# The summing DMA of a weight pair is issued four products after its loads, and its block is loaded first

## The chip, the core and the metric

The kernel runs on one core of a Trainium2 chip. The core has five engines that run side by side: TensorE (PE) multiplies, VectorE (DVE) and ScalarE (ACT) do the element-wise work, GpSimd (POOL) does a little of it and issues one kind of DMA, and SyncE (SP) issues nearly all other DMAs. Each engine works through its own queue in order and waits there for semaphores. The metric is the device time of one execution in microseconds (us), as the median over runs.

## The reference, cut to what matters

A trunk of four residual layers over 512 tokens of width 1024, in float32: pooling mixer, gated convolution, latent attention, pooling mixer. Nearly all of the time goes into products of the normalized activations with weight matrices; these three lines hold most of the weights:

```python
u, z = jnp.split(xn @ w_in, 2, axis=-1)        # pool_mixer, w_in 1024 x 4096, twice
b, c, h, z = jnp.split(xn @ w_in, 4, axis=-1)  # conv_mixer, w_in 1024 x 8192
h = xn @ w_in                                  # mla_mixer,  w_in 1024 x 2752
```

Each mixer ends in `(mixed * silu(z)) @ w_out` and is added to `x`; a last `rms_norm` closes the trunk.

## The kernel before

**Arithmetic.** Every float32 operand is split into a high part (a copy by ACT, rounded) and a low part (a subtraction by DVE); a product takes three matmuls (high x high, high x low, low x high), so every weight tile costs one ACT and one DVE pass before PE can read it.

**Chunks and pairs.** The work is a list of jobs in a `Stream`. A CHUNK job loads one weight tile of 128 x 1024 floats (`load_chunk`, 512 KB), splits it (`prepare_chunk`, L245 and L248) and multiplies it. A PAIR job computes two output tiles at once with seven products instead of eight (`seven`, by a Strassen-like scheme), from four quarter blocks of the weights and sums of them. There are 52 pairs: 6 in the first pooling layer, 30 in the convolution, 8 in attention's input projection, 8 in the last pooling layer. Each product of a pair is 12 matmuls of 256 columns; a chunk's tile is 24 matmuls of 512 columns.

**What a pair loads.** `load_pair` (L113 to L121) takes three tiles: `r` (1024 columns, L116), `r4` (512 columns, L117, named wq) and `s13` (1024 columns, shown as `s`). `s13` is to hold two sums. Two DMAs put the same quarter block into its two halves (L119, 256 KB each); then a DMA on GpSimd's queue (L120) reads the 512 KB of `r`'s source once more and adds them to `s13` in flight. That adding DMA must wait until both loads of `s13` have landed. `r` and `s13` are buffers of the same tag (wr, four buffers, which the chunks use too); `r4` has two buffers of its own.

**What is done with it.** `prepare_pair` hands the split out over two steps, by positions: position 4 ACT copies `r` (tile ah, L393), position 5 DVE subtracts (al, L396) and ACT copies `s13` (sh), position 6 DVE subtracts (sl) and ACT copies `r4` (ch), position 7 DVE makes cl and two further sums (`sums`, L399 and L400: the last reader of `s13`), positions 10 and 11, that is 2 and 3 of the next step, the copies and subtractions for th and tl (the last readers of `r`).

**What sets the order.** `Stream.step` runs job j. It first loads jobs j+1 and j+2 that are not loaded yet, then puts the preparation of job j+1 into a table of steps, `now`, and runs the job, which calls `now(0)`, `now(1)`, ... between its products: each call executes the entries up to that position. What is left is moved to the next step by minus 8. So a pair is loaded two steps ahead of its products and split in the step before them. PE, DVE and ACT execute in exactly that order (`manual_schedule`, ORDERED in L38). SP's and GpSimd's queues are not in that list: the tile framework orders them and hands out the buffers at compile time, so that an instruction may stand in the queue ahead of one that the code issues before it.

**What else is on GpSimd.** A 16-column memset per convolution tile (L714), the window sums of the pooling layers (`add` in `post_u`, L617, one to four per tile), sums of squares (L282), the power -1/2 of the norms (`rows`, L300), and the scaling of the softmax in attention (L1032).

Of the kernel before, what the change touches and what calls it, by code (L numbers as in the profile page):

```python
# [9 lines left out]
F32 = mybir.dt.float32  # L10
# [3 lines left out]
ALU = mybir.AluOpType  # L14
PSUM = bass.MemoryType.PSUM

P = 128
S = 512
# [15 lines left out]
CH = 1024  # L34
# [30 lines left out]
def trunk_kernel(ctx: ExitStack, tc: tile.TileContext, a):  # L65
    nc = tc.nc
    cp = ctx.enter_context(tc.tile_pool(name="cp", bufs=1))
    wp = ctx.enter_context(tc.tile_pool(name="wp", bufs=1))
# [6 lines left out]
    def nm(s):  # L75
        cnt[0] += 1
        return f"{s}_{cnt[0]}"
# [4 lines left out]
    def wt(s, tag, dt=F32R, w=CH):  # L82
        return wp.tile([P, CH], dt, tag=tag, name=nm(s), bufs=BUFS[tag])[:, :w]
# [10 lines left out]
    def f(t):  # L94
        return t.bitcast(F32)
# [16 lines left out]

    def load_pair(src):  # L113

        r, r4, s13 = wt("wr", "wr", F32), wp.tile([P, S], F32, tag="wq", name=nm("wq"), bufs=2), wt("s13", "wr", F32)
        nc.sync.dma_start(r, src[:, :CH])  # L116
        nc.sync.dma_start(r4, src[:, CH + S :])  # L117
        for q in range(2):
            nc.sync.dma_start(s13[:, q * S : (q + 1) * S], src[:, CH : CH + S])  # L119
        nc.gpsimd.dma_start(s13, src[:, :CH], accum_op=ALU.add)  # L120
        return r, r4, s13  # L121

    raw0 = {}

# [39 lines left out]
    class Steps:  # L164
# [3 lines left out]
        def __init__(self, at=()):  # L168
            self.at = dict(at)
# [15 lines left out]
    class Stream:  # L185
# [1 line left out]


        def __init__(self):
            self.jobs, self.at, self.later, self.raw, self.ready = [], 0, Steps(), {}, {}  # L190

        def add(self, kind, src, run):
            self.jobs.append((kind, src, run))
# [1 line left out]
        def load(self, j):  # L195
            if j < len(self.jobs) and j not in self.raw:
                kind, src, _ = self.jobs[j]
                self.raw[j] = kind[0](src) if kind else None

        def prepare(self, j):  # L200
            if j >= len(self.jobs) or j in self.ready:
# [12 lines left out]
        def step(self):  # L214
            j = self.at
            self.at += 1
            self.load(j + 1)
            self.load(j + 2)
            now, self.later = self.later, Steps()
            now.put(self.prepare(j + 1), 2 if self.jobs[j][0] is PAIR and self.jobs[j + 1 :] and self.jobs[j + 1][0] is not PAIR else 0, first=True)  # L220
            self.jobs[j][2](self.ready.pop(j, None), now)
            now(7)
            left, self.later = self.later, Steps()
            self.later.put(now.at, -8)
            self.later.put(left.at)
# [7 lines left out]
    def load_chunk(src, width=CH):  # L233
        raw = wt("wr", "wr", F32, width)
        nc.sync.dma_start(raw, src)
        return raw

    def prepare_chunk(raw, width=CH, pool=False):
        h, l = wt("wh", "wh", w=width), wt("wl", "wh", w=width)

        def high():
            if pool:
                nc.gpsimd.tensor_scalar(out=h, in0=raw, scalar1=1.0, scalar2=1.0, op0=ALU.mult, op1=ALU.mult)
            else:
                nc.scalar.activation(h, raw, AF.Copy)  # L245

        def low():
            (nc.gpsimd if pool else nc.vector).tensor_tensor(out=l, in0=raw, in1=f(h), op=ALU.subtract)  # L248

        return (h, l), {1: [high], 2: [low]}  # L250

    def wchunk(src, width=CH, pool=False):
        w, steps = prepare_chunk(load_chunk(src, width), width, pool)
        Steps(steps)(2)
        return w

# [129 lines left out]
    def prepare_pair(raw):  # L386
# [15 lines left out]
        def part(h, l, q):  # L402
# [6 lines left out]
                   11: [low(r[:, S:], th[:, :S], tl[:, :S]), low(r4, th[:, S:], tl[:, S:])]}  # L409

    PAIR, CHUNK = (load_pair, prepare_pair), (load_chunk, prepare_chunk)

    def product(w, xf, what, form, out, begin=False, end=False, after=None):
# [382 lines left out]
    def mla_layer(stream, xn, begin, cos_sin, nxt):  # L796
# [140 lines left out]
        def first_k(w, now):  # L937
# [7 lines left out]
            qk[0] = hold.pop("q0"), split(pk, "k")  # L945

        NARROW = (lambda src: load_chunk(src, 768)), (lambda raw: prepare_chunk(raw, 768))
        for i in range(KD):
            ly.pair(stream, a["mla_z"][i], (post_z, post_z), lambda i=i: then(i))
# [8 lines left out]
        def values(g):  # L958
            wh, wl = wchunk(wv[g])
            for tk in range(NT):  # L960
                pv = ps("pv")
                for k in range(2):
                    ts_ = slice(tk * P, (tk + 1) * P)
                    xh, xl = kvl[k]
                    c = slice(k * S, (k + 1) * S)
                    nc.tensor.matmul(pv, xh[:, ts_], wh[:, c], start=(k == 0), stop=False)
                    nc.tensor.matmul(pv, xh[:, ts_], wl[:, c], start=False, stop=False)
                    nc.tensor.matmul(pv, xl[:, ts_], wh[:, c], start=False, stop=(k == 1))
                vs[g, tk] = split(pv, "v")

        def qrope(g):
            wh, wl = wchunk(wq[8 + g], 768)
            ab = []
            for e in range(2):
                pa = ps("pa")
                mtile(pa, wh, wl, ql, kn=3, ktot=3, stride=2 * P, off=e * P)
                t = ut("qr")
                nc.scalar.activation(t, pa, AF.Copy)
                ab.append(t)
            A, B = ab  # L980
            t1, t2 = ut("t1"), ut("t2")
            nc.vector.tensor_tensor(out=t1, in0=A, in1=cos, op=ALU.mult)
            nc.vector.tensor_tensor(out=t2, in0=B, in1=sin, op=ALU.mult)
            nc.vector.tensor_tensor(out=t1, in0=t1, in1=t2, op=ALU.subtract)
            nc.vector.tensor_tensor(out=t2, in0=B, in1=cos, op=ALU.mult)
            nc.vector.tensor_tensor(out=A, in0=A, in1=sin, op=ALU.mult)
            nc.vector.tensor_tensor(out=t2, in0=t2, in1=A, op=ALU.add)
            parts = [*split(t1, "qa"), *split(t2, "qb")]
            order = [parts[0], parts[2], parts[1], parts[3]]
            for hh in range(4):  # L990
                st = ut("qrs", F32R)
                for q, src in enumerate(order):
                    nc.sync.dma_start(f(st)[32 * q : 32 * q + 32, :], f(src)[32 * hh : 32 * hh + 32, :])
                qrs[4 * g + hh] = st

        def stage_a(h):
            if h % 2 == 0:
                hold["q"] = wchunk(wq[h // 2], 768)
            if h % 4 == 0:
                hold["k"] = wchunk(wk[h // 4])  # L1000
            pq = ps("pq")
            mtile(pq, *hold["q"], ql, kn=3, ktot=3, stride=2 * P, off=(h % 2) * P)
            q = split(pq, "q")
            pk = ps("pk")
            mtile(pk, *hold["k"], kvl, kn=2, ktot=2, stride=4 * P, off=(h % 4) * P)
            qk[h] = q, split(pk, "k")
# [175 lines left out]
    w = a["pool_out1"]  # L1182
# [64 lines left out]
    for kk in range(4):  # L1247
        raw = wt("wr", "wr", F32)
# [3 lines left out]
    for i in range(NT):  # L1252
# [14 lines left out]
        r = sp.tile([P, 1], F32, tag="fr", name=nm("fr"))  # L1267
# [101 lines left out]
```

## Time and profile before

| | before |
|---|---|
| median of 3 runs (lowest to highest) | 1501.44 us (1498.5 to 1502.46) |
| the profiled execution: time, span, granted clock | 1502.28 us, 1500.5 us, 0.991 |
| PE, DVE, ACT, POOL busy | 97%, 72%, 46%, 17% |
| DMA queues' share of 16 engines: SP's, GpSimd's | 31.7%, 10.9% |
| HBM read, mean rate over the span | 173.70 MB, 117 GB/s |

The profiled execution's span runs from its first to its last instruction; 1.78 us of its time lie outside. The page cuts the span into 40 slices of 37.5 us and gives busy tenths of each: DVE stands at 8 or 9 tenths in most of slices 9 to 23, in which the convolution and attention's input projection run, and PE at 9 throughout. A busy PE is not PE at its peak, since the ends of its matmuls are modelled; waits of PE are read more sharply from its weight loads (PEld), each of which belongs to one matmul. In a timeline row stand the start, the duration, engine, line, operation, tile written and read, and in brackets how long the engine was idle before and who ended that.

### The profile page before, as it was taken

How to read it: one execution, taken by the hardware profiler on the slowest of the kernel's cores; microseconds unless marked ns; L12 is line 12 of the kernel's file. 1: busy time of each engine (PE TensorE's matmuls, PEld its weight loads, DVE VectorE, ACT ScalarE, POOL GpSimd, SP SyncE). 2: the span in 40 equal slices, each digit the busy share in tenths (PEclk: the TensorE clock that was granted, in tenths of full speed). 3: DMA queues.
4: the chain of work that ended last, by engine and by line, in shares of the span. 5: the costliest groups of instructions: out<-in, count | busy, mean ns of one | idle time of the engine just before them, and what ended most of it. 6: DMA issues, size and time to landing. Idle time of an engine off the chain costs nothing. (4 is left out here: it accounts for less than half of the span.)

```text
span 1500.5 us, 22412 instructions
## 1 busy us (share of the span) xinstructions
PE 1451.2 (97%) x8560; PEld 1273.3 (85%) x8560; DVE 1086.7 (72%) x1771; ACT 686.9 (46%) x1174; POOL 258.3 (17%) x291
## 2 busy tenths in 40 slices
PE   9999999999999999999999999999999999999997
PEld 7788797888999889999879988788888798888886
DVE  5885556659988878998688976667755487655854
ACT  4352233445554425555355655555633355323333
POOL 2413106021001000000211001121201122311502
PEclk9999999999999999999999999999999999999999
DMA  6243354325676457666236642122122434343431
GB/s 229 70 121 105 102 137 99 127 89 120 179 185 162 139 125 191 168 181 194 86 97 169 159 148 74 55 66 84 43 84 85 113 106 115 132 108 117 113 113 57
DMA packets 65147, 181.71 MB, mean 121 GB/s; under 512 B 8080, under 2 KB 8080, under 8 KB 65040
## 3 DMA queue, kind: packets, MB, share of 16 engines
q1 hardware_dynamic: 56688, 151.44, 31.7%
q0 software_dynamic: 7488, 27.27, 10.9%
q8 instruction: 67, 1.10, 0.3%
q10 hardware_dynamic: 864, 1.57, 0.3%
q14 instruction: 40, 0.33, 0.1%
HBM read 173.70 MB, written 2.10 MB: 117 GB/s over the span
## 5 line engine op out<-in xcount | busy, mean ns | idle before, releaser
L248 DVE TENSOR_TENSOR wl<-wr,wh 128x1024 fp32r<-128x1024 f32 (+1 forms) x140 | 173.1, 1236 | 55.9 <-ACT wh L245 54.7
L245 ACT ACTIVATE wh<-wr 128x1024 fp32r<-128x1024 f32 (+1 forms) x140 | 144.4, 1034 | 147.7 <-PE o L259 47.7
L260 PE MATMUL o<-yh,wl 128*128 128x512 f32 x384 | 151.3, 394 | 1.9 <-DVE wl L248 1.9
L259 PE MATMUL o<-yl,wh 128*128 128x512 f32 x384 | 151.3, 394 | 0.2 <-DVE yl L667 0.2
L258 PE MATMUL o<-yh,wh 128*128 128x512 f32 x384 | 150.9, 393 | 0.1
L260 PE MATMUL pt<-xh,wl 128*128 128x512 f32 x367 | 145.3, 397 | 4.0 <-DVE wl L248 4.0
L258 PE MATMUL pt<-xh,wh 128*128 128x512 f32 x367 | 146.2, 398 | 2.7 <-ACT wh L245 2.5
L259 PE MATMUL pt<-xl,wh 128*128 128x512 f32 x367 | 145.2, 396 | 0.6 <-DVE xl L349 0.6
L396 DVE TENSOR_TENSOR sl<-s,sh 128x1024 fp32r<-128x1024 f32 x52 | 65.4, 1259 | 35.2 <-ACT sh L393 32.8
L440 ACT ACTIVATE kept<-bv 128x256 f32<-128x256 f32 x52 | 19.9, 383 | 152.6 <-PE bv L426 90.7
L260 PEld LDWEIGHTS o<-yh,wl 128*128 128x128 f32 x384 | 72.1, 188 | 19.2 <-DVE wl L248 2.8
L260 PEld LDWEIGHTS pt<-xh,wl 128*128 128x128 f32 x367 | 69.5, 189 | 21.6 <-DVE wl L248 5.3
L259 PEld LDWEIGHTS o<-yl,wh 128*128 128x128 f32 x384 | 72.1, 188 | 17.2 <-DVE yl L667 0.5
L258 PEld LDWEIGHTS o<-yh,wh 128*128 128x128 f32 x384 | 72.1, 188 | 17.0 <-ACT yh L664 0.5
L258 PEld LDWEIGHTS pt<-xh,wh 128*128 128x128 f32 x367 | 69.5, 189 | 19.9 <-ACT wh L245 3.8
L259 PEld LDWEIGHTS pt<-xl,wh 128*128 128x128 f32 x367 | 69.5, 189 | 16.5 <-DVE xl L349 1.0
L120 POOL DMA_DIRECT2D s<-in_conv_in x30 | 26.0, 865 | 329.6 <-DMA s<-in_conv_in 105.4
L617 POOL TENSOR_TENSOR s<-u 128x527 f32<-128x527 f32 x32 | 50.0, 1562 | 180.6 <-DVE u L580 146.5
L282 POOL TENSOR_TENSOR sq<-sq,sq 128x512 f32<-128x512 f32 x25 | 39.6, 1585 | 211.3 <-ACT sq L276 210.9
L396 DVE TENSOR_TENSOR al<-wr,ah 128x1024 fp32r<-128x1024 f32 x52 | 64.1, 1233 | 14.2 <-ACT ah L393 12.1
L617 POOL TENSOR_TENSOR s<-s 128x525 f32<-128x525 f32 (+2 forms) x48 | 69.8, 1454 | 14.4 <-PE pm L259 11.1
L393 ACT ACTIVATE sh<-s 128x1024 fp32r<-128x1024 f32 x52 | 54.9, 1055 | 35.1 <-DMA s<-in_conv_in 17.8
(308 smaller groups left out, 4575.2 us busy)
## 6 DMA issues: line engine op xcount, KB each, us to landing
wr<-in_conv_in SPq DMA_DIRECT2D x34, 512.0 KB, 5.6
wr<-in_pool_out SPq DMA_DIRECT2D x32, 512.0 KB, 3.3
wr<-in_pool_u SPq DMA_DIRECT2D x30, 512.0 KB, 3.9
s<-in_conv_in SPq DMA_DIRECT2D x60, 256.0 KB, 4.6
s<-in_conv_in POOLq DMA_DIRECT2D x30, 512.0 KB, 6.2
wr<-in_pool_z SPq DMA_DIRECT2D x18, 512.0 KB, 4.0
wr<-in_pool_grp SPq DMA_DIRECT2D x16, 512.0 KB, 3.3
wr<-in_conv_out SPq DMA_DIRECT2D x16, 512.0 KB, 3.5
```

Source lines behind the costliest of these rows:

```text
L120: nc.gpsimd.dma_start(s13, src[:, :CH], accum_op=ALU.add)
L245: nc.scalar.activation(h, raw, AF.Copy)
L248: (nc.gpsimd if pool else nc.vector).tensor_tensor(out=l, in0=raw, in1=f(h), op=ALU.subtract)
L258: nc.tensor.matmul(out, ah, bh, start=first, stop=False)
L259: nc.tensor.matmul(out, ah, bl, start=False, stop=False)
L260: nc.tensor.matmul(out, al, bh, start=False, stop=last)
L282: eng.tensor_tensor(out=self.sum, in0=self.sum, in1=sq, op=ALU.add)
L393: return lambda: nc.scalar.activation(h, t, AF.Copy)
L396: return lambda: nc.vector.tensor_tensor(out=l, in0=t, in1=f(h), op=ALU.subtract)
L440: nc.scalar.activation(dst, src, AF.Copy)
L617: nc.gpsimd.tensor_tensor(out=nx[:, lo:], in0=cur[:, lo:], in1=cur[:, lo - d : S + PAD - d], op=ALU.add)
```

## The change

`load_pair` takes the buffer of `s13` first and issues the two loads of `s13` ahead of those of `r` and `r4`. It no longer issues the adding DMA itself, but returns it as an entry for position 4; `Stream.load` collects such entries in a table `loads`, and `step` puts them into `now` before it runs the job. So the DMA is handed to GpSimd when the running job has come to its position 4, instead of at the start of the step. `load_chunk` returns an empty table.

```diff
     def load_pair(src):
-        r, r4, s13 = wt("wr", "wr", F32), wp.tile([P, S], F32, tag="wq", name=nm("wq"), bufs=2), wt("s13", "wr", F32)
+        s13 = wt("s13", "wr", F32)
+        for q in range(2):
+            nc.sync.dma_start(s13[:, q * S : (q + 1) * S], src[:, CH : CH + S])
+        r, r4 = wt("wr", "wr", F32), wp.tile([P, S], F32, tag="wq", name=nm("wq"), bufs=2)
         nc.sync.dma_start(r, src[:, :CH])
         nc.sync.dma_start(r4, src[:, CH + S :])
-        for q in range(2):
-            nc.sync.dma_start(s13[:, q * S : (q + 1) * S], src[:, CH : CH + S])
-        nc.gpsimd.dma_start(s13, src[:, :CH], accum_op=ALU.add)
-        return r, r4, s13
+        return (r, r4, s13), {4: [lambda: nc.gpsimd.dma_start(s13, src[:, :CH], accum_op=ALU.add)]}
...
         def load(self, j):
             if j < len(self.jobs) and j not in self.raw:
                 kind, src, _ = self.jobs[j]
-                self.raw[j] = kind[0](src) if kind else None
+                self.raw[j], steps = kind[0](src) if kind else (None, {})
+                self.loads.put(steps)
...
             now, self.later = self.later, Steps()
+            now.put(self.loads.at)
+            self.loads = Steps()
             now.put(self.prepare(j + 1), 2 if self.jobs[j][0] is PAIR and self.jobs[j + 1 :] and self.jobs[j + 1][0] is not PAIR else 0, first=True)
```

More of the change, by code (lines that the diff above doesn't have):

```diff
@@ L189, in __init__ @@
         def __init__(self):
-            self.jobs, self.at, self.later, self.raw, self.ready = [], 0, Steps(), {}, {}
+            self.jobs, self.at, self.later, self.loads, self.raw, self.ready = [], 0, Steps(), Steps(), {}, {}
         def add(self, kind, src, run):
@@ L235, in load_chunk @@
         nc.sync.dma_start(raw, src)
-        return raw
+        return raw, {}
     def prepare_chunk(raw, width=CH, pool=False):
@@ L252, in wchunk @@
     def wchunk(src, width=CH, pool=False):
-        w, steps = prepare_chunk(load_chunk(src, width), width, pool)
+        w, steps = prepare_chunk(load_chunk(src, width)[0], width, pool)
         Steps(steps)(2)
```

## The prediction

> **What bounds the kernel now.** I read the page first, then who waits for whom, then the time lines of single steps.
>
> ```profile
> PE 1451.2 (97%) x8560; PEld 1273.3 (85%) x8560; DVE 1086.7 (72%) x1771; ACT 686.9 (46%) x1174; POOL 258.3 (17%) x291
> ```
>
> PE is the bound: every matmul stands, none is removed by the change, so only PE's waits can go. The question is which of them hang on the block that the adding DMA completes. The list of waits answers it:
>
> ```profile
> ACT sh L393 <- DMA s<-in_conv_in: 17.8, 7, 4.8
> ```
>
> ACT stands 17.8 us, in 7 steps, before the copy of the summed block (sh) until the adding DMA has landed. One such step, in the convolution, on SP, GpSimd, ACT and DVE:
>
> ```profile
> 402.42 0.33 SPq L116 DMA_DIRECT2D wr<-in_conv_in  x1
> 404.92 0.90 SPq L119 DMA_DIRECT2D s<-in_conv_in  x2
> ```
> ```profile
> 411.11 0.86 POOL L120 DMA_DIRECT2D s<-in_conv_in  x1 [9.93 <-DVE cl L396]
> 411.65 0.45 POOL L714 MEMSET ch<- 128x16 f32 x1
> ```
> ```profile
> 414.62 1.05 ACT L393 ACTIVATE ah<-wr 128x1024 fp32r<-128x1024 f32 x1
> 416.33 0.38 ACT L440 ACTIVATE kept<-bx 128x256 f32<-128x256 f32 x1 [0.66 <-PE bx L426]
> 420.22 1.06 ACT L393 ACTIVATE sh<-s 128x1024 fp32r<-128x1024 f32 x1 [3.50 <-DMA s<-in_conv_in]
> ```
> ```profile
> 421.31 1.23 DVE L396 TENSOR_TENSOR sl<-s,sh 128x1024 fp32r<-128x1024 f32 x1 [3.45 <-ACT sh L393]
> ```
>
> The chain is: r is issued at 402.42, the two loads of s13 only at 404.92, the adding DMA starts at 411.11 and lands at 420.22 (9.1 us), and ACT, free at 416.33 + 0.38 = 416.71, has waited 3.50 us, and DVE's subtraction (sl) behind it 3.45. What PE loses by it is read from its weight loads, in two stretches of the convolution that hold the worst of these steps:
>
> ```profile
> PEld bv L420 <- ACT sh L393: 2.2, 2, 1.2
> PEld bv L426 <- DVE sl L396: 1.9, 2, 1.0
> PEld bx L426 <- DVE tl L396: 1.3, 4, 0.4
> ```
> ```profile
> PEld bx L426 <- DVE tl L396: 1.8, 2, 1.1
> PEld bv L426 <- DVE sl L396: 0.9, 1, 0.9
> ```
>
> The first fence is 400 to 500 us, the second 590 to 700 us. The waits for sh and sl are the late block itself; those for tl follow in the next products, because DVE has fallen behind. Together 2.2 + 1.9 + 1.3 + 1.8 + 0.9 = 8.1 us.
>
> **The loads in the new order.** Why is s13 issued later than r? SP waits for buffers:
>
> ```profile
> SPq L116 <- DVE wr L399: 170.2, 32, 10.6
> SPq L119 <- DVE tl L396: 84.6, 32, 4.7
> ```
>
> r takes the buffer that comes free first (L399 is the last reader of an older s13), s13 the one that comes free later (tl is the last reader of an older r). Both have the same tag, so I expect them to change places: s13 at 402.42, r at 404.92. That is 2.5 us earlier for s13 in a convolution step. Nothing is added: the DMAs, their bytes and their issue times stay.
>
> ```profile
> L120 POOL DMA_DIRECT2D s<-in_conv_in x30: 857/862/917, 340.6 to 692.5; - x30
> ...
> DMA to landing us min/median/max: 5.4/6.2/9.1
> ```
> ```profile
> wr<-in_conv_in SPq DMA_DIRECT2D x34, 512.0 KB, 5.6
> ...
> s<-in_conv_in SPq DMA_DIRECT2D x60, 256.0 KB, 4.6
> ```
>
> From the first load of s13 to the start of the adding DMA passed 411.11 - 404.92 = 6.2 us, with r ahead of it on the same engines. So the adding DMA now starts at 402.42 + 6.2 = 408.6 at the latest, or at about 407 if only the median landing of 4.6 us counts. It lands 5.4 to 9.1 us after its start (all pairs), so between 412.4 and 417.7; with 408.6 and the median of 6.2 at 414.8, 1.9 us before ACT is free for it. In the worst combination a wait of 1.0 us is left of 3.50.
>
> **The hand-over four products later.** A step's rhythm:
>
> ```profile
> 412.00:424.00 12.00, 10.46 (x87) 10.05 (x86) 8.48 (x13) 5.48 (x9) 0.96 (x2) 1.00 0.69 158
> 434.00:444.00 10.00, 10.00 (x87) 10.00 (x86) 9.90 (x14) 5.49 (x9) 0.95 (x2) 1.00 0.70 184
> ```
>
> Undisturbed, 87 matmuls take 10 us, so a product of 12 takes 1.4 us and four 5.5 us. The loads go out when a buffer comes free, which is inside the step, so position 4 passes at 402.42 + 5.5 = 407.9 at the latest; the loads land at 407.0 and the DMA could start soon after. So even taken literally, the hand-over costs 0 to 0.9 us in a convolution step, and I take 0: GpSimd's queue is ordered at compile time, not by the products, and the only other work there is a memset of 0.45 us, which moves ahead of the DMA at no cost. No new wait is added; the DMA still waits for its two loads and, as the only thing queued behind it, the next memset.
>
> **r, now behind.** Issued at 404.92 instead of 402.42, r lands 5.6 us later at 410.5. Its first reader is ah at 414.62. The cover is 4.1 us; once used up, each further microsecond delays ah, sh and sl together. SP's r4 stays behind both.
>
> **Term A, convolution and attention's projection.** Of the 8.1 us I take 80%, 6.5. The reason for the rest is DVE: with 9.90 us busy of 10 in an undisturbed stretch, it becomes the next late engine, and small waits for tl will stay. Bounds: 0 (below) and 8.1.
>
> **Term B, first pooling layer.** Here the DMA waits for its loads in GpSimd's queue with a window sum behind it:
>
> ```profile
> 236.51 0.87 POOL L120 DMA_DIRECT2D s<-in_pool_z  x1 [2.06 <-DVE pll L631]
> ...
> 242.29 1.91 POOL L617 TENSOR_TENSOR s<-u 128x527 f32<-128x527 f32 x1 [3.29 <-DVE u L580]
> ...
> 248.41 0.87 POOL L120 DMA_DIRECT2D s<-in_pool_z  x1 [1.93 <-DMA s<-in_pool_z]
> 249.01 1.59 POOL L617 TENSOR_TENSOR s<-s 128x513 f32<-128x513 f32 x1
> ```
> ```profile
> 237.82 0.33 SPq L116 DMA_DIRECT2D wr<-in_pool_z  x1
> 243.31 0.80 SPq L119 DMA_DIRECT2D s<-in_pool_z  x2
> ```
> ```profile
> 254.49 0.19 PEld L426 LDWEIGHTS bx<-xh,al 128*128 128x128 f32 x1 [3.47 <-DVE al L396]
> ```
>
> The sum at 249.01 could have started 1.93 us before 248.41, so it is 2.5 us late; DVE forms the mean after it, then al, for which PE waits 3.47 us. With s13 at 237.82 the DMA starts at about 244.0 and is out of the way: 2.5 us gained. Bounds: 3.4 if the delay of the tile before (the idle 2.06 ahead of 236.51) goes too, and 0.2 if the DMA is queued ahead of the sum of 242.29 and holds it until 244.0 (1.7) and through its own issue (0.6).
>
> **Term C, last pooling layer.** The norm's power waits behind the DMA:
>
> ```profile
> 1190.36 0.08 DVE L295 DVE_READ_ACCUMULATOR2_ANT sv<- 128x1 f32 x1
> ```
> ```profile
> 1191.10 0.87 POOL L120 DMA_DIRECT2D s<-in_pool_z  x1 [12.44 <-DMA s<-in_pool_z]
> 1191.66 1.37 POOL L300 TENSOR_TENSOR sr<-sv,mhalf 128x4 f32<-128x4 f32 x1
> ```
> ```profile
> 1177.90 0.33 SPq L116 DMA_DIRECT2D wr<-in_pool_z  x1
> ```
> ```profile
> 1194.27 0.19 PEld L319 LDWEIGHTS pr<-dg,ones 128*128 128x128 f32 x1 [1.89 <-DVE dg L313]
> ```
>
> Its input is there at 1190.44. With s13 loaded at 1177.90 the DMA is issued by 1184.1, and the power starts 1.2 us (by its row, 1191.66) to 1.5 us (by the DMA's end, 1191.97) earlier: 1.3, of PE's wait of 1.89. Lower bound 0, if another late input shows.
>
> **Sum.** 6.5 + 2.5 + 1.3 = 10.3 us. The profiled execution took 1502.28 us, so it would take 1492.0; it lay 0.84 us above the median of 1501.44, so for the median I forecast 1491.1.
>
> **The rivals.**
>
> *The adding DMA gets longer as it gets earlier.* It now starts while r and r4 of its own pair are under way. The 9.1 us above belong to a DMA that overlapped the next r, issued at about the same time; the engines' share is 0.70 in the stretch of 434 to 444. If 9.1 became the rule instead of 6.2, the 2.5 us won by the loads would be used up, term A would be 0, and the time 1501.44 - 3.8 = 1497.6. For it speaks the spread of 5.4 to 9.1; against it, that by 408.6 r (404.92) has run for most of its 5.6 us, and that the next pair's loads now come after more of the DMA is done. The Trainium skill, "DMA: Bandwidth & Descriptors", section "Issuing engines are not separate DMA queues", says that DMAs of all issuing engines run on the same 16 DMA engines and interleave, so that using several queues saves only issue time. By that rule a reordering only chooses who is delayed, which is this rival; the spread in the row agrees with the rule, but leaves open whether r's 4.1 us of cover are enough to pay for it.
>
> *The change does not do what it says.* SP's and GpSimd's queues are ordered at compile time, and there the DMA's place may follow from when its inputs are ready, and the buffers from another rule than "first asked, first served". Then nothing moves: 1501.4. Against it: the two rows of SP's waits, 32 times each, which fit the order of asking in `load_pair`.
>
> *r becomes the late block (slower).* It decides from the point where r takes over 9.7 us (414.62 - 404.92) to land. If it came 1 us late in each of the 38 pairs of the convolution and the projection, ACT would wait 38 us. Today 17.8 us of waiting for sh cost PE the 8.1 us, or 0.46 each, so 38 x 0.46 = 17.3 us lost, 8.1 us of present waits replaced and B and C kept (3.8): 1501.44 + 17.3 - 8.1 - 3.8 = 1506.8. Against it: the medians, 4.1 us away.
>
> **How the numbers follow.** Chances: forecast 0.67; longer DMA 0.16; nothing moves 0.10; r late 0.07. A measurement of this kernel can tell about 0.3%, or 4.5 us, from no change: faster means below 1496.9. The forecast lies there nearly always (0.65 of its 0.67), the longer DMA on the edge (half, 0.08), so faster 0.73; same 0.02 + 0.08 + 0.10 = 0.20; slower 0.07. The range: below, all of A, B and C at their upper bounds, 8.1 + 3.4 + 1.5 = 13.0, or 1488.4, and a little for tl waits outside the two stretches: 1487. Above, 1499: it takes in the longer DMA and leaves out "nothing moves" and "r late", 0.17.
>
> **What would show it.** In the changed profile L119 of SP waits for L399 and L116 for tl; s13's loads stand ahead of r's. The wait of sh for the adding DMA falls from 17.8 us to under 4. The sums of L617 no longer stand behind a waiting L120, the power L300 follows its input at once, and PE's waits for sh, sl and al near 254 are gone while some for tl stay. The forecast is wrong if sh still waits (longer DMA), if ah shows waits for its load (r late), or if L116 still precedes L119 on SP.

## The result, and the profile after

| | before | after |
|---|---|---|
| median of 9 runs each | 1501.44 us | 1493.93 us |
| lowest to highest | 1498.5 to 1505.5 us | 1492.57 to 1497.19 us |
| ratio after/before, 95% interval | | 0.995 [0.9935, 0.9965] |
| the profiled execution: time, span, granted clock | 1502.28, 1500.5, 0.991 | 1493.1, 1491.3, 0.992 |

One of the nine executions of the changed kernel, 1579.66 us at a granted clock of 0.846, is in the median but left out of the ratio and of the lowest-to-highest row. The change makes the kernel faster, by 7.5 us between the medians and by 9.2 us between the two profiled spans, and the whole interval lies beyond the 0.3% that a measurement can tell. Line numbers from L220 of before on are 3 higher after (in the experiments they differ again); the adding DMA is L121, the loads of s13 L117, r L119, r4 L120.

The busy times of the page differ little from before. PE stays the bound:

```profile
PE 1446.5 (97%) x8560; PEld 1272.4 (85%) x8560; DVE 1086.2 (73%) x1771; ACT 683.8 (46%) x1174; POOL 255.7 (17%) x291
```

SP's list of waits after the change (engine and line, what ended the wait, us in total, times, longest) shows that r and s13 have changed places: s13's loads (L117) now wait for the last reader of an older s13 (L402, L399 of before), and r (L119) for tl.

```profile
SPq L117 <- DVE wr L402: 200.6, 32, 11.1
SPq L119 <- DVE tl L399: 63.7, 31, 4.2
```

The same step of the convolution as before, on SP, GpSimd and ACT (start, duration, engine, line, operation, tile written and read; in brackets the idle time ahead and who ended it):

```profile
401.86 0.80 SPq L117 DMA_DIRECT2D s<-in_conv_in  x2
404.35 0.33 SPq L119 DMA_DIRECT2D wr<-in_conv_in  x1
```
```profile
407.28 0.86 POOL L121 DMA_DIRECT2D s<-in_conv_in  x1 [9.09 <-DVE al L399]
```
```profile
414.81 1.05 ACT L396 ACTIVATE ah<-wr 128x1024 fp32r<-128x1024 f32 x1
416.53 0.38 ACT L443 ACTIVATE kept<-bx 128x256 f32<-128x256 f32 x1 [0.67 <-PE bx L429]
416.81 1.05 ACT L396 ACTIVATE sh<-s 128x1024 fp32r<-128x1024 f32 x1
```

The two loads of s13 go out 3.06 us earlier than before (401.86 against 404.92) and r 1.93 us later (404.35 against 402.42). The adding DMA starts at 407.28 and its landing is at 413.40 in the trace, so it is there 3.4 us ahead of sh, which now carries no bracket: ACT does not wait. That holds for all 52 pairs: before the copy sh<-s, the list of waits after names no DMA at all, and by the landings in the trace the block is there 1.9 to 17 us ahead of its copy. The loads of r are in by 408.99, 5.8 us ahead of ah at 414.81.

In the view of the adding DMA's line (duration in ns, least/median/most; then the time to landing), and in the page's list of DMA issues (KB each, median us to landing):

```profile
L121 POOL DMA_DIRECT2D s<-in_conv_in x30: 860/862/1092, 335.6 to 679.1; - x30
...
DMA to landing us min/median/max: 5.5/7.0/8.5
```
```profile
wr<-in_conv_in SPq DMA_DIRECT2D x34, 512.0 KB, 4.5
...
s<-in_conv_in SPq DMA_DIRECT2D x60, 256.0 KB, 3.9
```

The adding DMA takes 0.8 us longer in the median (6.2 before), its worst case is shorter (9.1 before), and the loads are quicker (5.6 and 4.6 before).

The two stretches of the convolution (us; busy time and count of PE, PEld, DVE, ACT, POOL; granted clock; DMA share; GB/s):

```profile
412.00:424.00 12.00, 12.00 (x104) 12.00 (x103) 11.89 (x18) 7.11 (x13) 0.86 (x1) 1.00 0.69 171
434.00:444.00 10.00, 10.00 (x87) 10.00 (x86) 9.93 (x16) 5.47 (x11) 0.86 (x1) 1.00 0.76 180
```

The first one has 104 matmuls in 12 us where there were 87. DVE is busy for 11.89 of 12 us, and PE nevertheless waits for nothing.

**Where the time went, by stages.** For every matmul I took the distance from its start to the next start, less the median distance for matmuls of its width in the same profile (0.232 us for 512 columns, 0.118 us for 256). Summed, this is what TensorE lost against its undisturbed pace. It fell from 71.1 to 61.9 us, by 9.2, which is the whole difference of the spans. By stretches, in us, with the experiments told below, each from its one profiled execution:

| | first pooling layer, 60 to 300 | convolution, 300 to 710 | projection, 710 to 892 | last pooling layer, its start, 1140 to 1250 | last pooling layer, the rest, 1250 to 1440 | everywhere |
|---|---|---|---|---|---|---|
| before | 18.6 | 14.3 | 7.3 | 1.8 | 5.6 | 71.1 |
| after | 19.6 | 4.2 | 7.1 | 0.4 | 8.3 | 61.9 |
| e1, order alone | 21.0 | 4.2 | 7.0 | 0.3 | 9.5 | 63.8 |
| e2, hand-over alone | 19.4 | 10.0 | 9.8 | 1.8 | 5.8 | 68.3 |
| e6, convolution and projection alone | 18.7 | 4.3 | 7.0 | 2.3 | 4.1 | 58.3 |
| e7, pooling layers alone | 19.6 | 10.0 | 10.0 | 0.3 | 9.3 | 72.0 |
| e5, after, DMA behind the sums | 16.4 | 4.1 | 7.1 | 0.4 | 4.2 | 54.3 |
| e8, e6 and DMA behind the sums | 15.6 | 4.0 | 6.9 | 1.5 | 4.1 | 56.2 |
| e4, after, DMA behind all sums | 20.0 | 4.3 | 7.0 | 1.7 | 8.1 | 63.4 |
| e3, after, no adding DMA | 15.5 | 4.1 | 6.9 | 0.3 | 2.9 | 51.0 |

So the convolution gave 10.1 us, and the start of the last pooling layer 1.4. The first pooling layer lost 1.0, and the rest of the last one 2.7. The stretches left out of the table make up the remainder.

**The start of the last pooling layer.** The norm's power now starts as soon as its input is there: GpSimd's bracket names the input (sv), no DMA stands ahead of it, and in the waits of PE's weight loads between 1180 and 1200 us 0.4 us is left of 1.89.

```profile
1174.35 0.87 POOL L121 DMA_DIRECT2D s<-in_pool_z  x1 [10.91 <-DVE fl L385]
1181.18 1.04 POOL L303 TENSOR_TENSOR sr<-sv,mhalf 128x4 f32<-128x4 f32 x1 [5.96 <-DVE sv L298]
```
```profile
PEld pr L322 <- DVE dg L316: 0.4, 1, 0.4
```

**The first pooling layer.** Here the gain that I had counted on is missing. SP, GpSimd (two places), DVE and PE's weight loads:

```profile
240.24 0.80 SPq L117 DMA_DIRECT2D s<-in_pool_z  x2
244.44 0.33 SPq L119 DMA_DIRECT2D wr<-in_pool_z  x1
```
```profile
225.60 2.20 POOL L620 TENSOR_TENSOR s<-s 128x525 f32<-128x525 f32 x2
229.89 0.87 POOL L121 DMA_DIRECT2D s<-in_pool_z  x1 [2.09 <-DMA s<-in_pool_z]
...
245.52 0.87 POOL L121 DMA_DIRECT2D s<-in_pool_z  x1 [8.21 <-DMA s<-in_pool_z]
246.13 1.36 POOL L620 TENSOR_TENSOR s<-u 128x527 f32<-128x527 f32 x1
```
```profile
232.12 0.18 DVE L626 TENSOR_TENSOR hd<-s,con 128x16 f32<-128x16 f32 x1 [1.97 <-POOL s L620]
...
239.00 1.21 DVE L251 TENSOR_TENSOR wl<-wr,wh 128x1024 fp32r<-128x1024 f32 x1
...
242.60 0.68 DVE L583 TENSOR_TENSOR u<-pt,R 128x512 f32<-128x512 f32 x1
...
251.18 0.17 DVE L626 TENSOR_TENSOR hd<-s,con 128x16 f32<-128x16 f32 x1 [4.83 <-POOL u L613]
```
```profile
255.03 0.19 PEld L429 LDWEIGHTS bx<-xh,al 128*128 128x128 f32 x1 [3.82 <-DVE al L399]
```

It begins two tiles earlier. The adding DMA at 229.89 stands inside that tile's chain of window sums and waits 2.09 us for its loads (in the kernel before it stood in the next tile's chain, at 236.51); DVE waits 1.97 us for the sums, and its subtraction wl ends at 239.00 + 1.21 = 240.21, where in the kernel before it ended at 236.57 + 1.22 = 237.79. That subtraction frees the buffer for which SP waits: s13 goes out at 240.24, as r did at 237.82 before. For the tile shown last, the input of the first window sum is ready at 242.60 + 0.68 = 243.28. The adding DMA now stands ahead of that sum in GpSimd's queue, waits there until its loads have landed, and the sum starts at 246.13, which is 2.85 us late. DVE waits 4.83 us for the sums, al comes after that, and PE waits 3.82 us for al (3.47 before).

**The end of the last pooling layer.** The same once more, on GpSimd and SP:

```profile
1382.40 1.39 POOL L620 TENSOR_TENSOR s<-s 128x525 f32<-128x525 f32 x1
1388.32 0.87 POOL L121 DMA_DIRECT2D s<-in_pool_z  x1 [4.52 <-PE pt L263]
1388.92 2.72 POOL L620 TENSOR_TENSOR s<-s 128x521 f32<-128x521 f32 x2
```
```profile
1379.34 0.80 SPq L117 DMA_DIRECT2D s<-in_pool_z  x2
```

A tile's chain of four window sums is cut after the second: the DMA waits 4.52 us between them. In the kernel before a DMA stood inside this chain too, but it waited only 1.20 us:

```profile
1393.83 0.87 POOL L120 DMA_DIRECT2D s<-in_pool_z  x1 [1.20 <-PE pm L259]
```

After the change the bracket names a product of PE, but the second load of s13 lands at 1387.75 in the trace, 0.57 us ahead of the DMA, the same distance as in the convolution, so it is the load that ends this wait. That load took 8.4 us beside r (1377.34) and the adding DMA of the pair before (1378.92 to 1387.30). The longest waits of PE's weight loads between 1392 and 1425 us follow. The first row was there before (2.1), the second was not, and of the third 0.2:

```profile
PEld bx L429 <- DVE tl L399: 2.1, 1, 2.1
PEld bv L429 <- DVE cl L399: 1.4, 1, 1.4
PEld bx L423 <- ACT kept L443: 1.4, 1, 1.4
```

### The profile page after: what moved, and what is told of

Read it like the earlier page. It is cut to its first block, busy times and chain, and to the rows that moved or that the text cites. A ratio compares the mean times of both kernels' runs of the same rounds, so it can differ in the third digit from the quotient of the medians.

```text
span 1491.3 us, 22421 instructions
## 1 busy us (share of the span) xinstructions
PE 1446.5 (97%) x8560; PEld 1272.4 (85%) x8560; DVE 1086.2 (73%) x1771; ACT 683.8 (46%) x1174; POOL 255.7 (17%) x291
## 5 line engine op out<-in xcount | busy, mean ns | idle before, releaser
L251 DVE TENSOR_TENSOR wl<-wr,wh 128x1024 fp32r<-128x1024 f32 (+1 forms) x140 | 172.3, 1231 | 56.2 <-ACT wh L248 55.7
L399 DVE TENSOR_TENSOR sl<-s,sh 128x1024 fp32r<-128x1024 f32 x52 | 64.6, 1242 | 21.5 <-ACT sh L396 19.3
L121 POOL DMA_DIRECT2D s<-in_conv_in x30 | 26.2, 872 | 310.0 <-DVE al L399 76.1
L399 DVE TENSOR_TENSOR al<-wr,ah 128x1024 fp32r<-128x1024 f32 x52 | 64.1, 1233 | 15.3 <-ACT ah L396 13.2
L620 POOL TENSOR_TENSOR s<-s 128x525 f32<-128x525 f32 (+2 forms) x48 | 66.4, 1384 | 14.5 <-PE pm L262 11.1
L1035 POOL TENSOR_SCALAR p<-p,sm 128x512 f32<-128x512 f32 (+1 forms) x64 | 34.0, 549 | 199.5 <-DVE sm L1034 139.1
```

Source lines behind the costliest of these rows:

```text
L121: return (r, r4, s13), {4: [lambda: nc.gpsimd.dma_start(s13, src[:, :CH], accum_op=ALU.add)]}
L399: return lambda: nc.vector.tensor_tensor(out=l, in0=t, in1=f(h), op=ALU.subtract)
L620: nc.gpsimd.tensor_tensor(out=nx[:, lo:], in0=cur[:, lo:], in1=cur[:, lo - d : S + PAD - d], op=ALU.add)
L1035: nc.gpsimd.tensor_scalar(out=pt[:, :w], in0=pt[:, :w], scalar1=sm_, scalar2=1.0, op0=ALU.mult, op1=ALU.mult)
```

## The experiments

The theory after the result: the order of the loads is all that acts. It takes the waits for sh out of the convolution, and in the pooling layers it puts the DMA in front of window sums. The rivals: the later hand-over does a part of it; the pooling layers' loss is one of the DMA traffic and not of GpSimd's queue. The first four runs share one set of runs of the kernel before (median 1500.67 us), the other four another (1501.65 us).

**e1_order_alone.** The order of the loads is kept, and the adding DMA is issued right behind them as before.

```diff
-        return (r, r4, s13), {4: [lambda: nc.gpsimd.dma_start(s13, src[:, :CH], accum_op=ALU.add)]}
+        nc.gpsimd.dma_start(s13, src[:, :CH], accum_op=ALU.add)
+        return (r, r4, s13), {}
```

> The new order of the loads, with the adding DMA issued in the code right behind them, as before the change, and not at position 4. If the order of the loads is the whole change (theory 1), this is the changed kernel over again: ratio to before 0.995 within 0.0015, sh never waits for the adding DMA in the convolution, the power of the last pooling layer follows its input within 0.2 us. If the later hand-over earns part of it (theory 2: it keeps GpSimd's queue free for other work), the time lies above that by 1.5 us or more (0.996 and up) and the power of the last pooling layer waits behind the adding DMA again.

Measured: 1495.1 us, ratio 0.9964 [0.9951, 0.9977]. In the trace the queues of SP and of GpSimd hold the same instructions in the same order as those of the changed kernel, sh waits for no DMA, and the table shows the same stretches won and lost. The hand-over four products later is a change of the source alone. The 1.2 us between the medians of the two can't be its effect, since the queues do not differ; it is scatter. The ratio alone would not have settled it: 0.9964 lies within 0.0015 of 0.995, as theory 1 expects, and also in the range of theory 2 (0.996 and up).

**e2_handover_alone.** The old order of the loads, with the adding DMA handed out at position 4.

```diff
-        s13 = wt("s13", "wr", F32)
-        for q in range(2):
-            nc.sync.dma_start(s13[:, q * S : (q + 1) * S], src[:, CH : CH + S])
-        r, r4 = wt("wr", "wr", F32), wp.tile([P, S], F32, tag="wq", name=nm("wq"), bufs=2)
+        r, r4, s13 = wt("wr", "wr", F32), wp.tile([P, S], F32, tag="wq", name=nm("wq"), bufs=2), wt("s13", "wr", F32)
         nc.sync.dma_start(r, src[:, :CH])
         nc.sync.dma_start(r4, src[:, CH + S :])
+        for q in range(2):
+            nc.sync.dma_start(s13[:, q * S : (q + 1) * S], src[:, CH : CH + S])
```

> The old order of the loads (r, r4, then s13), with the adding DMA handed over at position 4. Theory 1: the kernel before over again, ratio 1.000 within 0.0015, sh waits about 18 us in all for the adding DMA in the convolution. Theory 2: a gain of 1.5 us or more (0.999 and below) from the pooling layers, or a loss if the hand-over delays the DMA: each microsecond costs about half a microsecond in the steps where sh waits already.

Measured: 1499.73 us, ratio 0.9992 [0.9976, 1.0007]: no difference. Both queues are in the order of the kernel before. The waits of ACT are there again, but smaller than in the profile of before (17.8 us in 7 steps, the longest of which is not the block's alone, as the last section shows):

```profile
ACT sh L395 <- DMA s<-in_conv_in: 8.9, 7, 2.8
...
ACT sh L395 <- DMA s<-in_mla_z: 2.6, 2, 1.4
```

With the same queues these waits differ from one execution to the next, and so does what they cost: in the table the convolution and projection together lose 21.6 us before, 19.8 in e2 and 20.0 in e7, against 10.9 to 11.3 in all kernels with the new order there. Of the projection's share in e2 and e7, 1.7 us are a drop of the granted clock (last section).

**e6_conv_alone and e7_pool_alone.** A second function `load_pair_old` (the old `load_pair`, returning an empty table) serves one kind of layer. In e6 the pooling layers use it, in e7 the convolution and the projection; everything else is the changed kernel. The edit of e6, cut; in e7 `OLD` and `PAIR` change places in the line of `self.kind`.

```diff
+    OLD = (load_pair_old, prepare_pair)
...
-        def __init__(self, xn, at=(1, 3), gap=3):
+        def __init__(self, xn, at=(1, 3), gap=3, pool=False):
+            self.kind = OLD if pool else PAIR
...
-            stream.add(PAIR, src, run)
+            stream.add(self.kind, src, run)
...
-        ly = Layer(xn, at, 3 if pre is None else 6)
+        ly = Layer(xn, at, 3 if pre is None else 6, pool=True)
```

> The change for the pairs of the convolution and of attention's projection; the pairs of the two pooling layers are loaded and added as before. Theory 1, by the waits of TensorE in the two profiles: the convolution and the projection give 8 us (waits for sh, sl and the tl behind them), the pooling layers together cost 3 us in the changed kernel, so this one is about 8 us below before: 1493.4, ratio 0.9945, equal to the changed kernel or up to 3 us below it. If the gain of the convolution is given back in the layers behind it, the ratio is above 0.997.

> The change for the pairs of the two pooling layers alone; the convolution and the projection stay as before. Theory 1: 1.6 us gained at the power of the last pooling layer, 1.4 us lost around 250 us and 3 us lost at the end of the last pooling layer, where window sums stand behind an adding DMA that waits: 1 to 3 us slower than before, ratio 1.001 to 1.002. If the pooling layers gain what the prediction gave them (3.8 us), the ratio is 0.9975.

Measured: e6 1490.47 us, ratio 0.9935 [0.9918, 0.9952]; e7 1503.15 us, ratio 1.0016 [1.0003, 1.0029]. Against the median of before that is 10.2 us gained in the convolution and the projection, and 2.5 us lost in the pooling layers; the sum, 7.7 us, agrees with the whole change (7.5). The pooling layers' part is small: e7's interval excludes 1 by 0.0003 only. In the table e7 has the new order's gain at the start of the last pooling layer and its loss in the rest of it, and e6 has neither. In the first pooling layer they stand 0.1 (e6) and 1.0 us (e7) above before.

**e5_behind_sums.** The changed kernel; each adding DMA is bound behind the last window sum that was issued before its pair was loaded. The binding is on the order in GpSimd's queue alone and adds no wait. It has an effect only where there are window sums, in the pooling layers.

```diff
+    last_sum = []
...
-        return (r, r4, s13), {4: [lambda: nc.gpsimd.dma_start(s13, src[:, :CH], accum_op=ALU.add)]}
+        sums = last_sum[-1:]
+
+        def add():
+            i = nc.gpsimd.dma_start(s13, src[:, :CH], accum_op=ALU.add)
+            if sums:
+                tc.add_manual_dep(i.ins, sums[0].name, mybir.DependencyInfo(mybir.DependencyClass.NoSync, mybir.DependencyReason.DATA), reason="behind the sums")
+
+        return (r, r4, s13), {4: [add]}
...
-                    nc.gpsimd.tensor_tensor(out=nx[:, lo:], in0=cur[:, lo:], in1=cur[:, lo - d : S + PAD - d], op=ALU.add)
+                    last_sum.append(nc.gpsimd.tensor_tensor(out=nx[:, lo:], in0=cur[:, lo:], in1=cur[:, lo - d : S + PAD - d], op=ALU.add).ins)
```

> The changed kernel, with each adding DMA of the pooling layers bound to stand in GpSimd's queue behind the window sums that were issued before its loads. Theory 1 (the losses of the pooling layers come from sums that stand behind a waiting DMA): TensorE's waits near 250 us fall from 3.8 to under 1.5 us, those at the end of the last pooling layer from 5.3 to about 2 (what the kernel before had), so 4 to 6 us less than the changed kernel: 1488 to 1490, ratio 0.9915 to 0.993. Theory 3 (the sums are late for another reason, such as DVE and GpSimd disturbing each other or the transfers themselves): no change from 0.995.

Measured: 1486.47 us, ratio 0.9898 [0.9877, 0.9919], the fastest complete kernel here. It beats the kernel before and the changed kernel, whose interval ends at 0.9935. GpSimd near the place of the first pooling layer, and what PE's weight loads wait for between 240 and 262 us:

```profile
241.91 1.91 POOL L629 TENSOR_TENSOR s<-u 128x527 f32<-128x527 f32 x1 [5.27 <-DVE u L592]
243.89 3.56 POOL L629 TENSOR_TENSOR s<-s 128x525 f32<-128x525 f32 x3
247.40 0.11 POOL L622 MEMSET u<- 128x16 f32 x1
247.44 0.87 POOL L126 DMA_DIRECT2D s<-in_pool_z  x1
248.05 1.36 POOL L629 TENSOR_TENSOR s<-u 128x527 f32<-128x527 f32 x1
```
```profile
PEld bx L438 <- DVE al L408: 1.2, 1, 1.2
PEld bx L438 <- DVE tl L408: 1.0, 1, 1.0
PEld bv L438 <- DVE sl L408: 0.5, 1, 0.5
```

The sum follows its input (u), the DMA comes after it and no longer waits, and 1.2 us is left of the wait of 3.8 for al. The DMA is 1.9 us later than in the changed kernel (247.44 against 245.52), and still sh waits for no DMA. In the table the loss falls by 3.2 and 4.1 us in the two places, 7.3 of the 7.6 us between the two totals. That is more than the 4 to 6 us expected; 3.4 us of it are a clock that no longer drops (last section). The loads, bytes and DMAs are those of the changed kernel, so it was the place in the queue and not the amount of traffic.

**e8_conv_and_behind.** e6, with the same binding in `load_pair_old`: old order in the pooling layers, but behind the sums.

```diff
-        nc.gpsimd.dma_start(s13, src[:, :CH], accum_op=ALU.add)
+        i = nc.gpsimd.dma_start(s13, src[:, :CH], accum_op=ALU.add)
+        if last_sum:
+            tc.add_manual_dep(i.ins, last_sum[-1].name, mybir.DependencyInfo(mybir.DependencyClass.NoSync, mybir.DependencyReason.DATA), reason="behind the sums")
```

> The change in the convolution and the projection, the old order of loads in the pooling layers, and there each adding DMA bound to stand behind the window sums issued before it. Against the convolution alone (0.9935): theory 1 expects the wait near 250 us to shrink from 3.5 to about 1 (the sum no longer waits 2.5 us), the wait of 1.3 us for the power of the last pooling layer to stay, and no new one as long as the DMAs still land before ACT reads: 2 to 3 us less, ratio 0.9915 to 0.9925. Theory 3: 0.9935 again.

Measured: 1488.29 us, ratio 0.9908 [0.9888, 0.9928]. Against e6 the first pooling layer loses 3.1 us less (15.6 against 18.7). Of PE's 3.5 us for al between 240 and 262 us nothing is left in e8's list there (1.2 for kept and 1.0 for tl stand in it). So the old order paid there too; the change neither cured nor caused that wait, it only moved the place of the DMA in the queue. This rests on the two profiles: the intervals of e6 and e8 overlap. e5 and e8 can't be told apart (the intervals overlap): once the sums are free, the order of the loads matters little in the pooling layers.

**e4_behind_all.** The opposite question: does a late block cost more than a late window sum? The DMA is bound behind all window sums issued up to position 4, also those of the next tile. The edit as against e5:

```diff
         def add():
             i = nc.gpsimd.dma_start(s13, src[:, :CH], accum_op=ALU.add)
-            if sums:
-                tc.add_manual_dep(i.ins, sums[0].name, mybir.DependencyInfo(mybir.DependencyClass.NoSync, mybir.DependencyReason.DATA), reason="behind the sums")
+            if last_sum:
+                tc.add_manual_dep(i.ins, last_sum[-1].name, mybir.DependencyInfo(mybir.DependencyClass.NoSync, mybir.DependencyReason.DATA), reason="behind the sums")
```

> The changed kernel, with each adding DMA of the pooling layers put behind all window sums issued up to its hand-over at position 4, the next tile's included. This puts a price on a summed block that is late: by the profile the DMA of the pair used at 245 us would start at about 252 and land at about 258, 13 us after ACT wants it. Theory 1: ACT waits for it there and at the end of the last pooling layer, TensorE waits 8 to 12 us at each, ratio above 1.003. If lateness in the pooling layers is hidden (their pairs had 7 to 17 us to spare), the time stays below 0.998.

Measured: 1493.56 us, ratio 0.994 [0.9919, 0.9962], the same as the changed kernel. I had expected it to be slower than the kernel before, and that was wrong. ACT does wait long for the block, in three places, 11.60, 4.02 and 12.96 us. The first one, and what PE's weight loads wait for beside it, between 240 and 262 us:

```profile
255.67 1.06 ACT L403 ACTIVATE sh<-s 128x1024 fp32r<-128x1024 f32 x1 [11.60 <-issue]
```
```profile
PEld bv L430 <- ACT sh L403: 2.9, 1, 2.9
PEld bv L436 <- DVE sl L406: 1.0, 1, 1.0
```

The bracket names nobody, but the block lands at 255.52 in the trace, 0.15 us ahead of sh. Of the 11.60 us that ACT stands before sh, PE feels only 2.9 + 1.0, and of the 12.96 us 3.6 + 1.0. I had taken too much of the wait of ACT for a wait of PE. ACT is busy for less than half of the span, and in the pooling layers of the changed kernel the block is there 7.6 to 17 us ahead of its copy, so most of the wait is slack. And the 3.8 us for al went at the same time.

**e3_no_adding.** The changed kernel without the adding DMA. The products then use the plain quarter block in place of the sums; that part of the computation is left out.

```diff
-        return (r, r4, s13), {4: [lambda: nc.gpsimd.dma_start(s13, src[:, :CH], accum_op=ALU.add)]}
+        return (r, r4, s13), {}
```

> The changed kernel without any adding DMA: the sums that it makes are left out, so the kernel computes products with the plain block in their place. It shows what the adding DMA still costs. Theory 1: nothing in the convolution and the projection (TensorE's waits there stay as in the changed kernel, 3.5 us from 340 to 480 and none from 480 to 700), and the waits near 250 us and at the end of the last pooling layer shrink by some 6 us together: ratio 0.991. If the DMA's traffic still slows the rest, more than that: below 0.989.

Measured: 1483.11 us, ratio 0.9875 [0.9852, 0.9899]. It is the floor for everything that the adding DMA can still cost: 10.8 us below the changed kernel's median, about 3 below e5's. In the convolution (4.1 against 4.2) and the projection (6.9 against 7.1) nothing is left to win. Nearly all of it lay in the pooling layers: 4.1 and 5.4 us in their two places. I had expected some 6 us there, a ratio of 0.991, and below 0.989 if the DMA's traffic slows the rest as well. The ratio lies below. e5, which keeps the traffic, wins 7.6 of the 10.9 us between the totals, so the traffic can have at most the other 3.3; what they are was not tried.

## Why the prediction was right, and where it was not

**The sum.** 1491.1 us were forecast and 1493.93 measured, within the range, faster as expected. But the parts came out otherwise: one term was too small, one had the wrong sign, and one was not there at all. That the sum came so near is luck: by the table A gave 3.8 us more than forecast, B 3.5 us less, and the place without a term took 2.7.

**The order of the loads, the buffers.** Right. SP's waits are the two rows foretold, and in the step of the convolution the DMA landed at 413.40, where 412.4 to 417.7 with 414.8 as the middle had been worked out.

**The hand-over at 0.** Right, and for the reason given: the queues are ordered at compile time. e1 and e2 show that it does nothing whatever, neither cost nor gain.

**Term A, 6.5 us (0 to 8.1).** The mechanism was right, the size too small. The table gives 10.1 us for the convolution and 0.2 for the projection; e6 gives 10.2 between medians, or 7 to 12 by its interval. What failed is the factor of 80%. Its reason, that DVE "becomes the next late engine" and that small waits for tl stay, did not hold: DVE is busy for 11.89 of 12 us, and PE waits for nothing in these stretches. From 400 to 710 us the weight loads waited 8.9 us in all before (8.1 of them in the two stretches of the sum) and not at all after; the 4.1 us of waits at 340 to 400 us are the same in both. The other 1.2 of the 10.1 us no list of waits names. The full engine was not late here once its inputs were in time. e2 and e7 show besides that the size of this term is not a fixed number: 19.8 to 21.6 us in the convolution and the projection with the old order.

**Term B, 2.5 us (0.2 to 3.4).** Wrong, and this is the step that failed: "With s13 at 237.82 the DMA starts at about 244.0 and is out of the way". The buffers changed places, but the first one came free 2.4 us later than before, because an adding DMA had cut the window sums two tiles ahead; s13 came at 240.24. And in the queue the DMA was put ahead of the tile's first sum and not between the tiles. That is the mechanism of the lower bound ("queued ahead of the sum of 242.29"), but the start of the DMA had been priced at 244.0 and came at 245.52. The table gives a loss of 1.0 us in this pair of executions. Over the kernels with the old order there (18.6, 19.4, 18.7) and those with the new one (19.6, 21.0, 19.6) it is 1.2 in the mean: no gain, and a small loss.

**Term C, 1.3 us.** Right: 1.4 in the table, with the power following its input.

**What no term held.** The end of the last pooling layer lost 2.7 us (3.7 from before to e7), because the same queue was not looked at there. I priced two places where a DMA stood ahead of a sum or a power and did not ask at which other places it would now come to stand. e5 gives it back, 4.1 us. Nor did any term hold the clock that drops behind a wait.

**The rivals.** *Longer DMA*: true as to the fact, too small to matter. The adding DMA's median rose by 0.8 us of the 2.5 that it could have used up, and nothing waits for it. The Trainium skill, "DMA: Bandwidth & Descriptors", section "Issuing engines are not separate DMA queues", says that DMAs of all issuing engines interleave on the same 16 DMA engines. The rows agree in that one kind of DMA got longer and the others shorter: the adding DMA 0.8 us longer, r 1.1 and s13 0.7 shorter. *Nothing moves*: true for one half of the change (e2), false for the other (e1). *r late*: did not come; r lands 5.8 us ahead of its reader in the step shown, with 4.1 foreseen, and by the trace at least 3.2 us ahead in every pair.

## What to carry to other kernels

A DMA that waits for its own loads on a queue that also computes is a wait for all the computing behind it, so look up in the built queue what stands behind each such DMA, at every place, and bind it behind what is due first: that took this kernel from 0.995 to 0.9898 of the time before. Where a framework orders the queues, a later line in the source may be no change at all; compare the queues before pricing it. And price a late block at the engine that is the bound: 17.8 us of ACT's waits in the convolution stood for 8.9 us of PE's, 11.6 us in another layer for 3.9.

## What the runs showed of the hardware that was not expected

**A wait of TensorE is paid twice.** The granted clock (the third column from the right) drops after the waits in the pooling layers. Windows of 12 us that hold such a wait and what follows it, in the changed kernel, in e5 and in e1:

```profile
250.00:262.00 12.00, 8.38 (x52) 7.66 (x51) 10.72 (x13) 3.41 (x7) 7.78 (x6) 0.86 0.17 51
1404.00:1416.00 12.00, 7.69 (x50) 7.16 (x49) 11.30 (x15) 6.22 (x10) 3.75 (x3) 0.86 0.29 87
```
```profile
250.00:262.00 12.00, 9.87 (x74) 9.02 (x73) 11.89 (x17) 5.91 (x10) 5.04 (x3) 1.00 0.45 122
1396.00:1408.00 12.00, 10.43 (x81) 9.61 (x81) 9.40 (x15) 7.54 (x13) 3.96 (x4) 1.00 0.51 128
```
```profile
250.00:262.00 12.00, 8.02 (x39) 7.52 (x38) 9.81 (x11) 2.45 (x6) 8.62 (x7) 0.72 0.19 43
```

0.86 over 12 us is 1.7 us of clock lost, on top of the wait itself, and 0.72 is 3.4 us, twice that. In the changed kernel the clock was 0.50 from 256.20 to 259.62 us, and 1.00 in the 3.4 us on either side. Where the binding has cut the wait to 1.2 us or less, the clock stays at 1.00. So of the 3.2 and 4.1 us between the changed kernel and e5 in the two pooling places, 1.7 us each are the clock's, which no term of the prediction had. The Trainium skill, "TensorE: Matmul & The Clock Gate", section "Part 1: The HAM clock gate (the "warmup" mystery)", says that the clock falls to half after at least one idle window of about 3.4 us and comes back after a busy window of the same length. The size agrees: half of 3.4 is 1.7. The threshold does not agree: waits too short to hold such a window were followed by the drop at times. Near the end of the last pooling layer PE waits 2.1 us for tl in the kernel before, and 2.1 us in e6 as well. Windows of 8 us that begin there, first of before, then of e6:

```profile
1416.00:1424.00 8.00, 6.08 (x37) 5.88 (x38) 7.38 (x12) 3.95 (x6) 0.00 (x0) 0.79 0.21 76
```
```profile
1404.00:1412.00 8.00, 6.08 (x49) 5.67 (x48) 7.93 (x13) 4.33 (x7) 0.38 (x1) 1.00 0.29 98
```

The same wait was followed by the drop in one execution (8 us at 0.79, again 1.7 us) and by none in the other. So a wait of about 2 us may or may not be paid twice, and those of over 3 us for al in the first pooling layer (3.5 to 4.2 us in six kernels with and without the change) were in every profile. So were the 2.9 us for sh there in e4 (12 us at 0.86) and the 2.7 us for kept in the projection of e2 and e7 (8 us at 0.79).

**The same queues, other waits.** ACT's waits for the block in the convolution were 17.8 us in the profile of before and 8.9 in e2's, with identical queues of SP and GpSimd. The seven steps are not all the same ones. The longest of before, 4.83 us at 544.03, is put down to a product of PE (o) in e2 (4.67 us) and in the changed kernel (4.46 us, with the block there 6.3 us ahead), so it was not the block's alone; without it 13.0 us stand against 8.9. Why the DMAs of one execution are slower than those of another was not tried.
